# The decay-table spreads of a two-layer backbone, issued from ScalarE's DMA queue in place of GpSimd's

## The chip, the core and the metric

The kernel runs on one core of a Trainium2 chip. The metric is the device time of one execution in microseconds (us), as the median of several runs. Five engines work in parallel, each through its own instructions in a fixed order: TensorE (PE in the profile, with PEld for its weight loads), VectorE (DVE), ScalarE (ACT), GpSimd (POOL) and SyncE (SP). SP issues the loads of inputs and weights. A DMA is issued from the instruction list of one of these engines and is then carried out by the 16 DMA engines that all of them share.

## The reference, cut to what matters

The reference is a two-layer backbone on 256 latent tokens and 256 context tokens of width 1024. Each layer has an adaptive RMSNorm, three token mixers (a four-head retention in both directions, a short convolution, a multi-scale pooling), gates and an output projection, and then a hierarchical mixture of 16 experts. What the change touches is the decay of the retention:

```
rel = j[:, None] - j[None, :]
intra_decay = jnp.where(rel[None] >= 0.0,
                        jnp.exp(log_gamma[:, None, None] * jnp.maximum(rel, 0.0)[None]), 0.0)
scores = jnp.einsum('bnihd,bnjhd->bnhij', qc, kc) * intra_decay[None, None]
...
w_fwd = jnp.exp(log_gamma[0][:, None] * (n_tok - 1.0 - m)[None, :])
w_bwd = jnp.exp(log_gamma[1][:, None] * m[None, :])
```

Each score is multiplied by a power of the head's decay that depends only on the distance of the two tokens. So for each layer and head a row of 511 numbers (distances -255 to 255) is enough, and a second row of 511 for the decay from the context.

Ahead of the mixers, the conditioning `c @ w_ada[l] + b_ada[l]` gives shift, scale and gate; the mixers of layer 0 can't start without shift and scale.

## The kernel before, in words

All matrix products are done with operands split into a high and a low part: for each 128x1024 weight piece, ScalarE writes the rounded copy `wh` (L74) and VectorE the rest `wl` (L75), and TensorE does three products (L183 to L185). The pieces come in order through a ring of four buffers `raw` (L164, issued by SP); during the first stage ten more buffers `rawx` stand beside it.

**The first stage** (`src0`) runs before the first projection. `decays` computes the decay rows of all 8 layer-head pairs, 8 x 1022 numbers, and ACT writes them to `dg` in DRAM (L329). `ada_now` (L202 to L210) does four groups of the conditioning: 16 loads of 512 KB of `w_ada` (`in_wada`), issued by SP beside the input `x` (2 MB). Groups 0 and 2 come first, then `rstd`: squares, their sum, GpSimd's power (L371, `rs`) and VectorE's product of the whole input with it (L1293). Then follows `mix_norm0` for the first half of the 1024 channels: ACT's and DVE's `hf` (L430, L432), ACT's rounded copy `hT` (L433) and DVE's rest (L434). Groups 1 and 3 of the conditioning use split pieces (`wh`, `wl`); a row of each group is copied by ACT as `arow` (L205), turned by TensorE (L208) and added by DVE (`mod`, L210). When group 3 is in `mod`, `mix_norm0` does the second half. The last `hT` ends the stage. The whole order of each engine is fixed by a scheduler at build time.

**The decay tables.** `spread` (L333) copies the two rows of one layer and head 128 times in DRAM, from `dg` to `dw`: 256 rows of 2044 bytes, 511 KB. `table` (L340) then reads `dw` with a row step of 510 in place of 511 elements, so that each of the 128 partitions gets the row shifted by one: 384 KB into the tile `tab`. `scores` multiplies with `tab` (L563, L566, `pr`). There is one `tab` buffer for all heads, so each `table` waits until the scores of the head before are done.

`spread` is written in a block `tc.issue_after(mark[0].ins)`. `mark[0]` is the ScalarE instruction noted last: the `hT` copies of `mix_norm0`, the copies in `split`, a copy in `u_pool`. The first spread of layer 0 is written at the first head, the next three behind the first unit of heads 0 to 2, and the four of layer 1 one behind each `u_pool` of layer 0.

**The mixers** of layer 0 take up 75 to 560 us of the span; TensorE does one projection after the other there.

Of the kernel before, what the change touches and what calls it, by code (L numbers as in the profile page):

```python
# [78 lines left out]
def trunk(tc, io):  # L79
    nc = tc.nc  # L80
# [219 lines left out]
    ND = 2 * S - 1  # L300
    dg = dram.tile([NL * H, 2, ND], F32, name="dg")
    dw = dram.tile([NL * H, 2, P * ND], F32, name="dw")
# [30 lines left out]
    def spread(l, h):  # L333

        i = l * H + h
        with tc.issue_after(mark[0].ins):
            nc.gpsimd.dma_start(dw[i].rearrange("m (p j) -> p m j", j=ND),
                                dg[i].unsqueeze(0).to_broadcast([P, 2, ND]))

    def table(tab, l, h):  # L340
# [107 lines left out]
    def mixers(l, xsrc, x):  # L448
# [155 lines left out]
        for h in range(H):  # L604
            tab = hd.tile([P, 2, 384], F32, name="tab", tag="tab", bufs=1)
            if l == 0 and h == 0:
                spread(0, 0)
            table(tab, l, h)
            sg = []
            unit(u_qk, h, 0)  # L610
            if l == 0 and h < H - 1:
                spread(0, h + 1)
            if l == 0 and h == 0:
                late_consts()
            if last:
                for e in range(2):
                    unit(u_g, e, sg)
                    if h == 0:
                        late_norm(hd, range(4 * e, 4 * e + 4))
            unit(u_qk, h, 1)  # L620
            wv = [nextw(4), nextw(4)]
            after(DS[l], lambda tab=tab: scores(tab))
            after(DA[l], lambda h=h, sg=sg: attend(h, sg))
            for t2 in range(2):
                unit(u_v, t2, wv)
            if not last:
                for e in range(2):
                    unit(u_g, e, sg)
# [58 lines left out]
        for j in range(4):  # L687
            c = []
            unit(u_pool, j)
            if l == 0:  # L690
                spread(1, j)
            for i in range(3):
                unit(u_conv, j, i, c)
# [742 lines left out]
```

## Time and profile before

| what | value |
|---|---|
| median of 3 runs | 1699.37 us (1696.66 to 1704.01) |
| the profiled execution | 1695.72 us, of which the span is 1693.9 us |
| PE busy | 1623.9 us (96%) |
| DVE busy | 1348.3 us (80%) |
| ACT busy | 858.8 us (51%) |
| POOL busy | 69.9 us (4%) |
| DMA moved | 375.56 MB, mean 222 GB/s |

Busy times are those of the whole span. The page also cuts the span into 40 slices of 42 us: PE shows 5 and 7 tenths in the first two and 9 in most others, DMA 9 and 7 in the first two. Times in the rows further down are from the span's start; a row of the timeline gives start, duration, engine, line, what is written from what, and in brackets the idle time of the engine before it and what ended that.

### The profile page before, as it was taken

How to read it: one execution, taken by the hardware profiler on the slowest of the kernel's cores; microseconds unless marked ns; L12 is line 12 of the kernel's file. 1: busy time of each engine (PE TensorE's matmuls, PEld its weight loads, DVE VectorE, ACT ScalarE, POOL GpSimd, SP SyncE). 2: the span in 40 equal slices, each digit the busy share in tenths (PEclk: the TensorE clock that was granted, in tenths of full speed). 3: DMA queues.
4: the chain of work that ended last, by engine and by line, in shares of the span. 5: the costliest groups of instructions: out<-in, count | busy, mean ns of one | idle time of the engine just before them, and what ended most of it. 6: DMA issues, size and time to landing. Idle time of an engine off the chain costs nothing. (4 is left out here: it accounts for less than half of the span.)

```text
span 1693.9 us, 24511 instructions
## 1 busy us (share of the span) xinstructions
PE 1623.9 (96%) x8919; PEld 1367.7 (81%) x8919; DVE 1348.3 (80%) x2407; ACT 858.8 (51%) x1132; POOL 69.9 (4%) x101
## 2 busy tenths in 40 slices
PE   5799999999999997999999999999999989999996
PEld 1488888888888875888888878999999858888885
DVE  4577778977677458999999958779886688999995
ACT  3533332222222336777777745334444557787873
POOL 2000000000000001000000010000000010000000
PEclk8799999999999997999999999999999999999998
DMA  9733334454445526999999924435776579999991
GB/s 294 226 121 122 111 114 141 154 172 140 162 150 163 222 91 241 349 315 318 316 316 331 318 81 152 137 122 173 250 260 210 188 262 370 350 353 349 343 338 45
DMA packets 101870, 375.56 MB, mean 222 GB/s; under 512 B 11368, under 2 KB 11752, under 8 KB 101488
## 3 DMA queue, kind: packets, MB, share of 16 engines
q1 hardware_dynamic: 95472, 348.74, 59.9%
q0 software_dynamic: 5248, 19.92, 3.8%
q10 hardware_dynamic: 1024, 5.28, 0.8%
q8 instruction: 72, 1.18, 0.3%
q14 instruction: 54, 0.44, 0.1%
HBM read 369.67 MB, written 8.41 MB: 223 GB/s over the span
## 5 line engine op out<-in xcount | busy, mean ns | idle before, releaser
L74 ACT CAST wh<-raw 128x1024 fp32r<-128x1024 f32 x319 | 332.5, 1051 | 482.0 <-PE mm L184 274.7
L75 DVE TENSOR_TENSOR wl<-raw,wh 128x1024 fp32r<-128x1024 f32 x319 | 385.0, 1219 | 70.3 <-ACT wh L74 65.0
L74 ACT CAST wh<-rawx 128x1024 fp32r<-128x1024 f32 x247 | 257.3, 1053 | 114.0 <-PE mm L185 76.2
L183 PE MATMUL mm<-hT,wh 128*128 128x512 f32 (+1 forms) x896 | 307.4, 344 | 2.9 <-ACT wh L74 2.8
L75 DVE TENSOR_TENSOR wl<-rawx,wh 128x1024 fp32r<-128x1024 f32 x247 | 293.2, 1218 | 18.7 <-ACT wh L74 15.5
L184 PE MATMUL mm<-hT,wh 128*128 128x512 f32 (+1 forms) x896 | 306.4, 343 | 0.0
L185 PE MATMUL mm<-hT,wl 128*128 128x512 f32 (+1 forms) x896 | 304.8, 341 | 0.0
L230 DVE SCALAR_TENSOR_TENSOR acc<-raw,sv,acc 128x256 f32<-128x256 f32 x462 | 196.9, 476 | 8.9 <-DMA raw<-in_wada_dram 8.9
L183 PE MATMUL mm<-wh,X 128*128 128x512 f32 x512 | 200.6, 392 | 0.7 <-issue 0.7
L184 PE MATMUL mm<-wl,X 128*128 128x512 f32 x512 | 200.2, 391 | 0.0
L185 PE MATMUL mm<-wh,X 128*128 128x512 f32 x512 | 199.5, 390 | 0.0
L183 PEld LDWEIGHTS mm<-hT,wh 128*128 128x128 f32 x896 | 169.9, 190 | 21.8 <-ACT wh L74 3.6
L185 PEld LDWEIGHTS mm<-hT,wl 128*128 128x128 f32 x896 | 170.1, 190 | 19.1 <-issue 0.5
L184 PEld LDWEIGHTS mm<-hT,wh 128*128 128x128 f32 x896 | 170.1, 190 | 18.7 <-issue 0.7
L183 PEld LDWEIGHTS mm<-wh,X 128*128 128x128 f32 x512 | 96.4, 188 | 20.9 <-issue 1.3
L184 PEld LDWEIGHTS mm<-wl,X 128*128 128x128 f32 x512 | 96.4, 188 | 20.4 <-DVE wl L75 1.2
L185 PEld LDWEIGHTS mm<-wh,X 128*128 128x128 f32 x512 | 96.1, 188 | 19.8
L183 PE MATMUL mm<-wh,aTh 128*128 128x512 f32 x256 | 103.3, 404 | 5.4 <-ACT aTh L74 5.1
L184 PE MATMUL mm<-wl,aTh 128*128 128x512 f32 x256 | 100.3, 392 | 0.0
L185 PE MATMUL mm<-wh,aTl 128*128 128x512 f32 x256 | 96.3, 397 | 0.0
L1104 PE MATMUL yy<-GT,y 128*128 128x512 f32 (+1 forms) x384 | 94.2, 361 | 2.2 <-DVE xT L1108 2.1
L1104 PEld LDWEIGHTS yy<-GT,y 128*128 128x128 f32 x384 | 66.6, 188 | 14.5 <-issue 1.7
(346 smaller groups left out, 2613.6 us busy)
## 6 DMA issues: line engine op xcount, KB each, us to landing
rawx<-in_wmoe_dram SPq DMA_DIRECT2D x244, 512.0 KB, 5.3
raw<-in_wmix_dram SPq DMA_DIRECT2D x176, 512.0 KB, 3.9
raw<-in_wmoe_dram SPq DMA_DIRECT2D x140, 512.0 KB, 5.4
raw<-in_wada_dram SPq DMA_DIRECT2D x82, 512.0 KB, 3.8
rawx<-in_wada_dram SPq DMA_DIRECT2D x14, 512.0 KB, 12.4
dw<-dg POOLq DMA_DIRECT2D x8, 511.0 KB, 25.6
tab<-dw POOLq DMA_DIRECT2D x8, 384.0 KB, 4.0
h2d<-xs ACTq DMA_DIRECT2D x6, 512.0 KB, 5.3
```

Source lines behind the costliest of these rows:

```text
L74: nc.scalar.copy(hi, src)
L75: nc.vector.tensor_sub(lo, src, hi.bitcast(F32))
L183: nc.tensor.matmul(out, st[0], mv[0], start=start, stop=False)
L184: nc.tensor.matmul(out, st[0], mv[1], start=False, stop=False)
L185: nc.tensor.matmul(out, st[1], mv[0], start=False, stop=stop)
L230: nc.vector.scalar_tensor_tensor(acc[v], w[:, k], s, acc[v], op0=OP.mult, op1=OP.add)
L1104: nc.tensor.matmul(p_, y[i][:, c], GT, start=gi == 0 and i == 0, stop=gi == ng - 1 and i == 1)
```

## The change

One line: the DMA of `spread` is issued from ScalarE's instruction list and no longer from GpSimd's. `table` stays with GpSimd.

```
     with tc.issue_after(mark[0].ins):
-        nc.gpsimd.dma_start(dw[i].rearrange("m (p j) -> p m j", j=ND),
+        nc.scalar.dma_start(dw[i].rearrange("m (p j) -> p m j", j=ND),
                             dg[i].unsqueeze(0).to_broadcast([P, 2, ND]))
```

The place of the eight spreads in the program moves with it. On GpSimd before, from the program's start to the first two tables (`dl`, `tokid` are constants; the memsets are edges of the pooling and convolution tiles):

```order
L317 IOTA dl 8x511
L125 IOTA tokid 128x4
L337 DMA dw<-dg 128x2x511 x5
L371 TENSOR_TENSOR rs<-ms,neghalf 128x4
L337 DMA dw<-dg 128x2x511 x3
L342 DMA tab<-dw 128x2x384
L657 MEMSET b_2000 128x2x8
L658 MEMSET b_2000 128x2x8
L638 MEMSET u 128x2
L639 MEMSET u 128x2
L342 DMA tab<-dw 128x2x384
```

All eight spreads stand around the power `rs` of the first norm. On GpSimd after the change, the same stretch:

```order
L317 IOTA dl 8x511
L125 IOTA tokid 128x4
L371 TENSOR_TENSOR rs<-ms,neghalf 128x4
L657 MEMSET b_2000 128x2x8
L658 MEMSET b_2000 128x2x8
L638 MEMSET u 128x2
L639 MEMSET u 128x2
L342 DMA tab<-dw 128x2x384 x2
```

The eight spreads are gone from GpSimd, and the first table stands behind the four memsets. On ScalarE at the end of the first stage, the difference (`hT_97` is the rounded half of `hT`, `qr` and `yc_361` are pieces of q and k of head 0):

```order
 L433 CAST hT_97<-hf 128x512 x2
-L74 CAST wh<-raw 128x1024 x2
+L337 DMA dw<-dg 128x2x511
+L74 CAST wh<-raw 128x1024
 L514 CAST qr_407<-mm 128x256
-L74 CAST wh<-raw 128x1024
+L74 CAST wh<-raw 128x1024 x2
 L514 CAST yc_361<-mm 128x256
+L337 DMA dw<-dg 128x2x511
 L514 CAST qr_452<-mm 128x256
 L514 CAST yc_361<-mm 128x256
```

The first spread stands directly behind the last `hT` of the stage, the second some copies later, among those of head 0. The other six follow one by one: two among the copies of heads 1 and 2, and four each behind a copy of `u_pool` (L660). Besides, a `wh` changes places with the copy `qr_407`. SP's order is the same as before.

## Rows read from the trace of the kernel before

**Rows 1.** Busy time by stretch; columns named in the first row.

```profile
core 0: us, PE busy (x) PEld busy (x) DVE busy (x) ACT busy (x) POOL busy (x), PEclk, DMA share, GB/s
10.00:20.00 10.00, 8.90 (x27) 2.41 (x26) 5.91 (x9) 4.77 (x8) 2.67 (x4) 1.00 1.00 415
25.00:45.00 20.00, 6.90 (x18) 2.03 (x17) 8.28 (x16) 1.04 (x1) 3.70 (x4) 0.61 1.02 220
75.00:560.00 485.00, 482.34 (x2488) 410.74 (x2487) 373.47 (x787) 137.30 (x189) 7.49 (x19) 1.00 0.44 143
```

**Rows 2.** Timeline of GpSimd, 0 to 110 us.

```profile
17.33 3.70 POOL L337 DMA_DIRECT2D dw<-dg  x5 [15.85 <-DMA dg<-ev]
...
26.58 2.11 POOL L337 DMA_DIRECT2D dw<-dg  x3
73.61 0.74 POOL L342 DMA_DIRECT2D tab<-dw  x1 [44.91 <-DMA raw<-in_wmix_dram]
```

**Rows 3.** DMA queues, 20 to 60 us: packets, MB, share of 16 engines.

```profile
q1 hardware_dynamic: 1532, 5.70, 55.5%
q0 software_dynamic: 896, 4.19, 43.5%
```

**Rows 4.** Timeline of SP's queue, 0 to 110 us: the last first-stage loads.

```profile
18.95 1.59 SPq L164 DMA_DIRECT2D rawx<-in_wada_dram  x2
```

**Rows 5.** Timeline of ScalarE, 0 to 110 us.

```profile
46.98 1.04 ACT L74 CAST wh<-raw 128x1024 fp32r<-128x1024 f32 x1 [12.99 <-DMA raw<-in_wada_dram]
47.93 1.58 ACT L430 ACTIVATE hf<-x,mod,sca 128x256 f32<-128x256 f32 x3
...
53.17 1.05 ACT L74 CAST wh<-raw 128x1024 fp32r<-128x1024 f32 x1 [1.61 <-DMA raw<-in_wada_dram]
...
56.74 1.04 ACT L74 CAST wh<-rawx 128x1024 fp32r<-128x1024 f32 x1 [1.53 <-DMA rawx<-in_wada_dram]
59.30 1.05 ACT L74 CAST wh<-rawx 128x1024 fp32r<-128x1024 f32 x1 [1.51 <-DMA rawx<-in_wada_dram]
61.05 1.04 ACT L74 CAST wh<-raw 128x1024 fp32r<-128x1024 f32 x1 [0.71 <-DMA raw<-in_wmix_dram]
62.54 0.30 ACT L123 CAST swr<-con 128x128 fp32r<-128x128 f32 x1 [0.44 <-DMA con<-in_con_dram]
63.88 1.04 ACT L74 CAST wh<-raw 128x1024 fp32r<-128x1024 f32 x1 [1.04 <-DMA raw<-in_wmix_dram]
64.83 0.57 ACT L205 COPY arow<-mm 4x512 f32<-4x512 f32 x1
66.42 1.04 ACT L74 CAST wh<-raw 128x1024 fp32r<-128x1024 f32 x1 [1.01 <-DMA raw<-in_wmix_dram]
...
71.63 0.62 ACT L433 CAST hT<-hf 128x512 fp32r<-128x512 f32 x1 [0.18 <-DVE hf L432]
```

**Rows 6.** Timeline of VectorE, 0 to 100 us.

```profile
27.82 4.87 DVE L1293 TENSOR_TENSOR x<-x,st 128x512 f32<-128x512 f32 x8 [2.00 <-PE st L381]
32.61 0.16 DVE L266 SCALAR_TENSOR_TENSOR sca<-mod,vec 128x8 f32<-128x8 f32 x1
34.02 1.23 DVE L75 TENSOR_TENSOR wl<-raw,wh 128x1024 fp32r<-128x1024 f32 x1 [1.25 <-ACT wh L74]
...
50.04 1.90 DVE L434 TENSOR_TENSOR hT<-hf,hT 128x512 fp32r<-128x512 f32 x3 [13.51 <-ACT hT L433]
...
92.03 0.68 DVE L563 TENSOR_TENSOR pr<-st,tab 128x512 f32<-128x512 f32 x1
```

**Rows 7.** The spreads (L337), from issue to landing.

```profile
DMA to landing us min/median/max: 11.2/25.6/31.1
```

**Rows 8.** The tables, 60 to 140 us, from issue to landing.

```profile
DMA to landing us min/median/max: 3.7/3.8/3.8
```

**Rows 9.** DMAs that ScalarE issued, tile `h2d`: ns min/median/max.

```profile
L870 ACTq DMA_DIRECT2D h2d<-xs x6: 326/328/747, 635.7 to 1357.3; - x6
```

**Rows 10.** Waits, 75 to 360 us: total us, times, longest.

```profile
ACT wh L74 <- DMA raw<-in_wmix_dram: 2.8, 2, 1.8
```

## The prediction

> **What bounds the kernel now.** I read the busy time by stretch first, since the page's average (PE 96%) hides where TensorE is not busy. From 75 to 560 us it is busy 482.34 of 485 us, and DMA has a share of 0.44 [rows 1]: the mixers are bound by TensorE. The first stage is not. From 25 to 45 us TensorE is busy 6.90 of 20 us, VectorE 8.28 and ScalarE 1.04, while the DMA engines are full (1.02) and yet move only 220 GB/s, against 415 GB/s, also full, from 10 to 20 us [rows 1]. So the second question was what the DMA engines do there. GpSimd's timeline shows the eight spreads going out from 17.33 to 28.7 us [rows 2], and the queues between 20 and 60 us show two users: SP's loads, 5.70 MB in 55.5% of the time of 16 engines, and the spreads, 4.19 MB in 43.5% [rows 3]. The spreads thus take 0.435 x 40 = 17.4 us of all 16 engines, 2.2 us each, and SP's bytes take 22.2 us where 415 GB/s would need 13.7 us. Third, what waits for this: ScalarE's timeline. Its copy at 46.98 us had stood 12.99 us for a load of `w_ada`; later copies of this stage waited 1.61, 1.53, 1.51, 0.71, 0.44, 1.04 and 1.01 us for loads too [rows 5]. All of the first stage's loads were issued by 20.5 us [rows 4], so they were late in flight and not late in issue. Nothing that needs a spread waits in this stage: the first table is issued at 73.61 us [rows 2], the first product with it starts at 92.03 us [rows 6]. The spreads are early by tens of microseconds and are paid for by loads that are not.
>
> **The change, part by part.**
>
> *Removed from the first stage: 4.19 MB of spreads.* By the order, none is issued before the last `hT` of the stage, which ended at 71.63 + 0.62 = 72.25 us [rows 5]. What SP has in flight at 20 us then runs by itself. Even if I charge it with all of SP's 5.70 MB [rows 3], which includes pieces for the mixers, at 415 GB/s [rows 1] it is through by 20 + 13.7 = 33.7 us; the pieces that ScalarE wants first are near the front of that.
>
> What is late next is VectorE: the product of the input with the norm's power runs from 27.82 us, and `sca`, which the first `hf` need, ends at 32.61 + 0.16 = 32.77 us [rows 6]. Nothing in this chain waits for a load. So the `hf` that started at 47.93 us [rows 5] start at 32.77 us: 15.2 us earlier. If the two copies ahead of them should come with the last of the 5.70 MB, at 33.7 us and 1.04 us each, the `hf` start at 35.8 us, and 12.1 us are left; that is the lower end of this term.
>
> From there to `arow` at 64.83 us ScalarE took 16.9 us, 6.8 us of it waiting for loads (the first six waits named above) [rows 5]. Not all of that comes back, as VectorE follows behind: from the first rounded `hT`, some 2.1 us after the `hf` begin, it has 1.90 us of `hT`, four `wl` of 1.23 us, another `hT` and a `mod` [rows 6], about 7.7 us, which ends at 42.6 us at the earliest; TensorE's products with the last piece come behind that, in the same order as before. I give these and the waits of three engines for each other 2 to 4 us, so `arow` stands at 44.6 to 46.6 us instead of 64.83 - 15.2 = 49.6 us. The term lies between 0 and 6.8 us; I take 3 us, the lower end of what the walk leaves.
>
> Behind `arow` there is one more wait of 1.01 us [rows 5], and TensorE's granted clock, 0.61 in the starved stretch [rows 1], which is its lower level of 1.2 GHz for most of it; whether it is higher in a denser stage no row tells. I set both at nothing, with 2 us to either side. Sum of the first stage: 15.2 + 3 = 18.2 us.
>
> *Added to ScalarE: eight issues.* The nearest row is ScalarE's own issue of 512 KB, 0.33 to 0.75 us [rows 9]: 2.6 to 6.0 us in all. ScalarE is busy 137.30 of 485 us in the mixers [rows 1], so nothing of it reaches TensorE as long as a `wh` is ready before its turn. Behind the first issue are queued a `wh` and the copy `qr` of head 0, behind the second the copy of k; TensorE waits for these only if the copies come later than its products before them. I take 0; if all of it were on the path, 6 us. The first spread waits for `dg`, long since landed; the second stands behind a load that SP issued many microseconds earlier. GpSimd loses eight issues of some 0.7 us at a time when little waits for it.
>
> *Moved into the mixers: the eight transfers.* Each takes 2.2 us of all DMA engines, 17.4 us together, in a stretch whose DMA share is 0.44 and where ScalarE's copies waited for mixer pieces only 2.8 us in 285 [rows 1, 3, 10]. I take 0, up to 3 us. Weighed against this is the Trainium skill (DMA: Bandwidth & Descriptors, Queues, rings and completion order): each DMA engine takes turns between the queue rows that have work, so a piece in flight beside a spread gets about half the engine, wherever the spread was issued. The trace agrees (220 GB/s beside the spreads, 415 before). By that rule the sum would be the one above only while the pieces are ahead of their use, and at most 17.4 us smaller if none is; that is the bound that the last rival goes beyond.
>
> *Added wait: the first table.* It was ready long before, and now hangs on a spread that goes out at about 72.25 - 18.2 = 54.1 us. Before, the last `hT` and the first product with the table were 92.03 - 72.25 = 19.8 us apart [rows 5, 6], and that distance is TensorE's work, which stays. In it must fit the issue (0.5 us), the landing of the spread, GpSimd's issue of the table (0.74 us) [rows 2] and its landing (3.8 us) [rows 8]: 14.8 us are left for the spread. Its landing took 11.2 us at best, 25.6 us in the median [rows 7], but that was with seven others and the loads in full engines; the best is the nearest to one spread alone. So the table is in time, by 3.6 us at least. By the Trainium skill's fit for one DMA (same page, Anatomy of one DMA), 2.0 us plus bytes over 436 GB/s, a spread alone would land in an estimated 3.2 us, and the slack would be 11.6 us; no row here shows a spread alone. The other tables wait for the scores of the head before, and their spreads go out a head earlier or more.
>
> So the profiled execution, 1695.72 us, becomes 1677.5 us. The median of the runs lies 3.65 us above that execution; against it I forecast 1699.4 - 18.2 = 1681.2, **1681 us**.
>
> **Rivals.**
>
> *The table takes the place of the load.* ScalarE's spread lands as late as the eight did in the median, 25.6 us: the scores wait 25.6 - 14.8 = 10.8 us, and with the worst, 31.1 us, 16.3 us. The gain shrinks to 7.4 or 1.9 us: 1692 to 1697.5 us. For it: the spread writes to DRAM in 2044-byte rows, and the weight pieces run beside it. Against: one spread needs 2.2 us of the engines. 9%.
>
> *The loads are slow by themselves.* If what remains in the stage runs at the 247 GB/s of 9.89 MB in 40 us that all users had together [rows 3], SP's 5.70 MB take 23 us instead of 40, the last copies end at 43 us instead of 60, and what ScalarE wants in the middle gains about half of the 18 us: 1690 us. For it: DMA was full in both stretches. Against: 415 GB/s with the same kind of loads just before. 8%.
>
> *The spreads hurt where TensorE is the bound* (slower). From 75 us on every microsecond that a weight piece is late counts in full, once its lead over its use is gone; before, the lead sufficed. If a spread costs there what it cost in the first stage in elapsed time, 40 us for eight, 5 us each, the mixers lose 40 us, and the net is 22 us slower: 1721 us. It decides from 18.2 / 8 = 2.3 us of TensorE's time per spread, which is just what one spread takes of the engines; a ScalarE held by each issue for that long, with the `wh` behind it, would do the same. Against: a DMA share of 0.44, four buffers ahead, and issues below 0.75 us. 7%.
>
> *The change does not do what it says*: it does, by the order; the eight stand on ScalarE.
>
> **How the numbers follow.** The forecast has 76%, with its own range from 1675 (the second term whole, 2 us from the clock) to 1688 us (first term at 12.1, the second at nothing, a little lost to the issues); the rivals have 9, 8 and 7%. About 0.5%, 8.5 us, is what a measurement of this kernel can tell from no change, so faster means below 1691 us: the forecast and half of the second rival, 80%. No change holds the first rival and the other half, 13%. Slower holds the last, 7%. The range that leaves out 2 in 10 goes from 1675 to 1693 us: it takes in the forecast's own and the nearer part of the first two rivals.
>
> **What would show it.** Right: between 25 and 45 us of the changed kernel no spread, the GB/s near 400 until all loads are in, no wait of ScalarE for `w_ada` above 2 us, the `hf` near 33 us, the last `hT` near 54 us, the first spread right behind it and the first `pr` near 74 us with TensorE and not the table ending its wait; from there on both traces the same distance apart, and 482 of 485 us of TensorE again. Wrong: `pr` waiting for the table (first rival), loads still late with the engines empty of spreads (second), gaps of TensorE at the places of the eight spreads or an issue on ScalarE above 2 us (third). Of the terms, the 3 us between `hf` and `arow` is the weakest.

## The result and the profile after

| kernel | median of its runs | range | ratio to the kernel before, 95% interval |
|---|---|---|---|
| before, beside it | 1698.01 us | 1696.27 to 1704.01 | |
| changed | 1681.01 us | 1673.98 to 1683.32 | 0.9887 [0.9848, 0.9926] |

The changed kernel is faster by 17.0 us at the median (forecast: 18.2). The profiled execution took 1683.32 us, its span 1681.5 us against 1693.9.

First the DMA engines from 20 to 60 us, in 40 slices of 1 us: their busy share in tenths, what they moved, and the queues (answering to [rows 3]).

```profile
DMA  9999999996000003899998994997603846848988
GB/s 410 401 414 414 410 401 410 418 406 270 20 0 0 0 0 74 332 428 423 311 381 332 406 414 176 299 332 184 238 29 41 303 180 121 215 135 176 279 221 114
...
q1 hardware_dynamic: 2541, 9.36, 64.4%
q10 hardware_dynamic: 368, 0.72, 8.5%
```

SP's loads run at 401 to 418 GB/s and are through at 30 us; then the engines have nothing to do until 35 us. Of the spreads, now on q10, only 0.72 MB is left here, behind 51.8 us; the 4.19 MB on q0 are gone. The stretch that answers to [rows 1], and two later ones:

```profile
core 0: us, PE busy (x) PEld busy (x) DVE busy (x) ACT busy (x) POOL busy (x), PEclk, DMA share, GB/s
25.00:45.00 20.00, 15.39 (x54) 5.80 (x53) 17.98 (x28) 11.35 (x17) 1.93 (x1) 0.83 0.68 260
75.00:560.00 485.00, 481.76 (x2439) 409.68 (x2439) 362.68 (x769) 132.50 (x181) 7.51 (x19) 0.99 0.47 153
105.00:110.00 5.00, 3.05 (x24) 2.88 (x23) 5.00 (x13) 2.03 (x5) 0.00 (x0) 0.92 0.49 159
```

From 25 to 45 us TensorE is busy 15.39 instead of 6.90 us, ScalarE 11.35 instead of 1.04. ScalarE's timeline (answering to [rows 5]):

```profile
27.21 1.04 ACT L74 CAST wh<-raw 128x1024 fp32r<-128x1024 f32 x1 [1.51 <-DMA raw<-in_wada_dram]
33.41 1.58 ACT L430 ACTIVATE hf<-x,mod,sca 128x256 f32<-128x256 f32 x3 [5.16 <-DVE sca L266]
...
45.57 0.57 ACT L205 COPY arow<-mm 4x512 f32<-4x512 f32 x1 [2.56 <-PE mm L202]
...
51.77 0.62 ACT L433 CAST hT<-hf 128x512 fp32r<-128x512 f32 x1 [0.18 <-DVE hf L432]
51.80 0.63 ACTq L337 DMA_DIRECT2D dw<-dg  x1
```

The copy that had stood 12.99 us for a load now stands 1.51 us, and what ends the wait ahead of the `hf` is VectorE's `sca`. The `arow` waits for TensorE and no longer for loads. GpSimd's first table, VectorE's `sca` and its first product with that table (answering to [rows 2, 6]):

```profile
58.94 0.96 POOL L342 DMA_DIRECT2D tab<-dw  x1 [5.40 <-DMA dw<-dg]
```

```profile
33.22 0.15 DVE L266 SCALAR_TENSOR_TENSOR sca<-mod,vec 128x8 f32<-128x8 f32 x1
...
71.74 0.68 DVE L563 TENSOR_TENSOR pr<-st,tab 128x512 f32<-128x512 f32 x1
```

The product starts 20.29 us earlier than before and is not made to wait by the table, which landed at 68.1 us. It is late by VectorE's own order: VectorE had stood 3.03 us, up to 65.50 us, for a load of `w_ada` that SP issued at 57.38 us, 0.4 us behind the second spread, and works from there to the product without a pause. TensorE waits 0.87 us for the product:

```profile
65.50 0.62 DVE L228 TENSOR_SCALAR acc<-raw,sv 128x256 f32<-128x256 f32 x2 [3.03 <-DMA raw<-in_wada_dram]
```

```profile
72.56 0.35 PE L183 MATMUL st<-yc 128*128 128x256 f32 x1 [0.87 <-DVE pr L563]
```

In again, the second run of this kernel below, these two waits are 2.31 and 0.16 us. The spreads' own rows, issue (ns) and landing (answering to [rows 7, 9]):

```profile
L337 ACTq DMA_DIRECT2D dw<-dg x8: 537/538/633, 51.8 to 299.6; - x8
DMA to landing us min/median/max: 7.1/7.2/7.5
```

The landing of the first table, 20 to 60 us:

```profile
tab<-dw POOLq DMA_DIRECT2D x1, 384.0 KB, 9.2
```

The first stage gains 19.9 us (end of the last `hT`: 72.25 before, 52.39 after). The span gains 12.4 us. So this execution gives 7.5 us back: the first product behind the mixers (L771) starts at 550.13 us, 18.2 us earlier than before (568.30), which leaves 1.7 us lost in the mixers and 5.8 us behind them. The next rows show a loss in the mixers: in turn ScalarE's issue of the third spread, SP's load that meets it, VectorE, which wants this load, and TensorE.

```profile
91.00 0.54 ACTq L337 DMA_DIRECT2D dw<-dg  x1
```

```profile
92.22 0.33 SPq L164 DMA_DIRECT2D raw<-in_wada_dram  x1
```

```profile
98.63 0.48 DVE L230 SCALAR_TENSOR_TENSOR acc<-raw,sv,acc 128x256 f32<-128x256 f32 x1 [2.84 <-DMA raw<-in_wada_dram]
...
107.91 0.68 DVE L598 TENSOR_TENSOR yf<-st,sg 128x512 f32<-128x512 f32 x1
```

```profile
108.73 0.47 PE L529 MATMUL st<-qr,swr 128*128 128x256 f32 x2 [1.95 <-DVE yf L598]
```

The spread goes out at 91.00 us and the load at 92.22; VectorE's accumulation for a later group of the conditioning stands 2.84 us for it, the `yf` behind it in VectorE's order comes late, and TensorE waits 1.95 us. It is busy 3.05 of the 5 us from 105 on, and its granted clock is 0.92 there.

Behind the mixers the loss goes with the clock. The row of the changed kernel, and that of before around the same products:

```profile
548.00:568.00 20.00, 20.00 (x97) 17.47 (x96) 7.04 (x15) 6.04 (x11) 0.00 (x0) 0.74 0.80 309
```

```profile
566.00:586.00 20.00, 20.00 (x125) 17.61 (x124) 8.29 (x17) 7.79 (x13) 0.00 (x0) 1.00 0.87 342
```

TensorE is busy all the time in both, but the clock is 0.74 in one: a stretch of 10.2 us at the lower level of 1.2 GHz, which begins right behind the small products of L771. Before ran the same products at 1.00. At half the clock 10.2 us are worth up to 5.1 of the 5.8 us (an estimate). Further on both kernels have stretches at the lower level: 36 us in all behind the mixers of before, 53 us in the changed kernel, these 10.2 us among them.

### The profile page after: what moved, and what is told of

Same layout as the page of the kernel before. It is cut to its first block, busy times and chain, and to the rows that moved or that the text cites. A ratio compares the mean times of both kernels' runs of the same rounds, so it can differ in the third digit from the quotient of the medians.

```text
span 1681.5 us, 24507 instructions
## 1 busy us (share of the span) xinstructions
PE 1626.4 (97%) x8919; PEld 1373.0 (82%) x8919; DVE 1347.9 (80%) x2407; ACT 858.1 (51%) x1132; POOL 64.1 (4%) x93
## 5 line engine op out<-in xcount | busy, mean ns | idle before, releaser
L1104 PEld LDWEIGHTS yy<-GT,y 128*128 128x128 f32 x384 | 66.6, 188 | 14.5 <-issue 1.7
```

Of the source, the lines that this page charges most:

```text
L1104: nc.tensor.matmul(p_, y[i][:, c], GT, start=gi == 0 and i == 0, stop=gi == ng - 1 and i == 1)
```

## The experiments

Two theories. **A**: only the place in time counts; the spreads took the DMA engines' time from the first stage's loads, and any late issue cures it. **B**: GpSimd's queue itself is the price, and another queue the cure.

Milestones of the profiled executions, in us; "mixers" runs from the last `hT` to the first L771, "rest" from there to the end of the span:

| kernel | early spreads | end of last hT | first L771 | span | mixers | rest |
|---|---|---|---|---|---|---|
| before | 8 | 72.25 | 568.30 | 1693.9 | 496.1 | 1125.6 |
| changed | 0 | 52.39 | 550.13 | 1681.5 | 497.7 | 1131.4 |
| again | 0 | 51.55 | 546.83 | 1673.8 | 495.3 | 1127.0 |
| nospread | none at all | 50.75 | 543.70 | 1669.1 | 493.0 | 1125.4 |
| pool_late2 | 0 | 52.34 | 550.08 | 1681.3 | 497.7 | 1131.2 |
| half | 4 | 60.44 | 552.67 | 1683.7 | 492.2 | 1131.0 |
| double | 16 | 97.28 | 591.48 | 1716.7 | 494.2 | 1125.2 |
| gap3 | 3, of ScalarE | 53.06 | 545.61 | 1675.2 | 492.6 | 1129.6 |
| idle1 | 1, of ScalarE | 53.64 | 546.35 | 1671.3 | 492.7 | 1125.0 |

**The change again, in more runs** (again; no edit).

> The changed kernel once more. In its first trace the first product with a table came 20.3 us earlier than before, but the span was only 12.4 us shorter: 3.3 us went near 105 to 113 us of the span (a gap of TensorE of 2 us, then 3.4 us of the lower clock), some 5 us in a stretch of 10.2 us at the lower clock from 553 to 563 us. If the first loss belongs to the third spread (its transfer beside a load of w_ada), it stands here again at the same place, 3 to 4 us. If the second is chance of the clock, it is absent or elsewhere here, and the span is 1676 to 1678 us; if it belongs to the change, it is here again and the span is 1680 to 1683 us. Median of the runs 1677 to 1683 us.

Measured 1675.76 us (1673.83 to 1678.28), ratio 0.9882 [0.9858, 0.9906], a little below the 1677 to 1683 us that I had expected. The wait of TensorE near 107 us is there again, and belongs to the change:

```profile
106.87 0.48 PE L529 MATMUL st<-qr,swr 128*128 128x256 f32 x2 [1.89 <-DVE yf L598]
```

The low clock right behind the mixers lasts 3.4 us here and not 10.2, and the rest takes 1127.0 us instead of 1131.4 with the same program: that part varies between executions.

**The spreads late, but from GpSimd** (pool_late). The edit is against the kernel before: a small GpSimd instruction reads the ScalarE copy that `mark` names, and the spread is issued behind it.

```
+    probe = cst.tile([P, 8], F32, name="probe")
...
-        i = l * H + h
-        with tc.issue_after(mark[0].ins):
+        i = l * H + h; late = nc.gpsimd.tensor_scalar(probe[:, i:i + 1], mark[1][:, 0:1], 0.0, None, op0=OP.mult)
+        with tc.issue_after(late.ins):
             nc.gpsimd.dma_start(dw[i].rearrange("m (p j) -> p m j", j=ND),
...
```

> All spreads stay in GpSimd's queue, as before, but each is issued only when the ScalarE copy is done behind which the change put it (a small GpSimd instruction that reads that copy's result stands ahead of each spread). Theory A, the place in time is what counts: hf near 33 us, last hT near 53 us, time 1678 to 1685 us, as with the change. Rival B, the queue is what counts (a spread from the software queue holds the DMA engines longer than one from ScalarE's): in the mixers the spreads then land later than 7.2 us, the first table is late, and at least half of the gain is missing: 1690 us or more.

Measured 1688.74 us, ratio 0.9949 [0.9932, 0.9967]: at first sight half of B. But its first stage was as short as the change's (the last `hT` ends at 50.44 us), and most of the loss lay in the mixers, 505.2 us against 495.3 in again, without a gap that holds it: products of 512 columns followed each other every 233 ns from 400 to 540 us, 227 ns in all kernels before. The tile `probe` takes 32 bytes of each partition and moves the tiles allocated behind it by as much, so the run told nothing about queues. It was repeated without the tile:

```
-    probe = cst.tile([P, 8], F32, name="probe")
-        i = l * H + h; late = nc.gpsimd.tensor_scalar(probe[:, i:i + 1], mark[1][:, 0:1], 0.0, None, op0=OP.mult)
+        i = l * H + h; late = nc.gpsimd.tensor_scalar(se[:, i, 0:1], mark[1][:, 0:1], 0.0, None, op0=OP.mult)
```

> The same as pool_late (all eight spreads back in GpSimd's list, each behind the ScalarE copy that holds it in the changed kernel), but the one number per partition that the small GpSimd instruction writes goes into a tile that exists already (se, not used any more at that time), so no tile of the kernel changes its address. Theory A (only the place in time matters, not which engine issues): first hf near 33 us, last hT near 51 us, matmuls in the mixers again 227 ns apart as in all kernels but pool_late, and 1674 to 1682 us. Theory B (GpSimd's queue itself costs, and with it the slower matmuls of pool_late): 233 ns apart again and 1686 to 1692 us.

Measured 1680.07 us (1677.35 to 1683.20), ratio 0.9891 [0.9868, 0.9913], as the change's 0.9887; the milestones are the change's within 0.2 us. The landing of its spreads and their first issue from GpSimd:

```profile
DMA to landing us min/median/max: 6.3/6.9/7.6
```

```profile
53.11 0.99 POOL L337 DMA_DIRECT2D dw<-dg  x1
```

A holds and B falls: late from GpSimd is worth the same as late from ScalarE. On GpSimd `issue_after` with a ScalarE copy had set no order (the eight spreads stood around `rs`); on ScalarE it does. That is how a change of queue became one of place. The meeting of the third spread with a load is there with GpSimd too: the spread goes out from GpSimd at 91.48 us, SP's load at 91.52, and TensorE waits 2.59 us for `yf`.

**No spreads** (nospread). The tables are read from `dg` and not from `dw`; nearly as many bytes as before.

```
-            nc.scalar.dma_start(dw[i].rearrange("m (p j) -> p m j", j=ND),
-                                dg[i].unsqueeze(0).to_broadcast([P, 2, ND]))
...
-        src = dw[l * H + h, :, P - 1:P - 1 + P * (ND - 1)].rearrange("m (p j) -> p m j", j=ND - 1)
+        src = dg[l * H + h].unsqueeze(0).to_broadcast([P, 2, ND])
```

> No spreads at all: the tables are read from the 511-number rows themselves, each partition the same row, 384 KB as before, so the scores are multiplied by a wrong table. All else stands where it stood. This is the price of what the change leaves in the mixers. If the third spread costs 3.3 us there and the others nothing: 1677 to 1679 us, no gap of TensorE near 105 us. If the moved spreads cost nothing: the time of the changed kernel, 1681 us. If all eight cost as much as the third: under 1665 us.

Measured 1672.54 us (1670.99 to 1673.37), ratio 0.9863 [0.9832, 0.9894]. That lies in none of the three ranges, which I had counted from the first 1681 us. What the eight late spreads still cost is some 3 us of the median of again. TensorE has no gap near 105 us:

```profile
105.00:110.00 5.00, 5.00 (x42) 4.91 (x41) 2.91 (x6) 2.37 (x4) 0.00 (x0) 1.00 0.18 71
```

The order of TensorE's work is no rival for the gap: it is the same from the first instruction to the last in pool_late2, which has the gap, and in nospread, which has not.

**Twice the spreads, early** (double; one copy of the two is read by nobody; the edit is against the kernel before).

```
-            nc.gpsimd.dma_start(dw[i].rearrange("m (p j) -> p m j", j=ND), ...
+            for d in (dw2, dw):
+                nc.gpsimd.dma_start(d[i].rearrange("m (p j) -> p m j", j=ND), ...
```

> The kernel before with each of the eight spreads written twice, the second time to a tensor that nobody reads: 16 transfers at the old early place, from GpSimd. Theory A (the price in the first stage is the time that the spreads take of the DMA engines, 2.2 us each): eight more cost 17 us or somewhat more there, the first wait for a load of w_ada ends near 60 to 65 us, and the whole takes 1712 to 1722 us. Rival (the price is GpSimd's early issues, or the loads are slow by themselves): below 1706 us, since the engine waits for nothing in that stage.

Measured 1718.74 us (1717.11 to 1719.78), ratio 1.0123 [1.0100, 1.0146]: 20 us more than before, as A says. ScalarE's waits for loads:

```profile
33.09 1.04 ACT L74 CAST wh<-raw 128x1024 fp32r<-128x1024 f32 x1 [8.12 <-DMA raw<-in_wada_dram]
47.02 1.04 ACT L74 CAST wh<-raw 128x1024 fp32r<-128x1024 f32 x1 [12.88 <-DMA raw<-in_wada_dram]
...
63.22 1.04 ACT L74 CAST wh<-rawx 128x1024 fp32r<-128x1024 f32 x1 [5.78 <-DMA rawx<-in_wada_dram]
72.84 1.04 ACT L74 CAST wh<-rawx 128x1024 fp32r<-128x1024 f32 x1 [8.58 <-DMA rawx<-in_wada_dram]
```

One detail was expected wrongly: the first long waits end where they did before (33 and 47 us), not at 60 to 65. The later copies pay instead, at 63 and 73 us. The same row of DMA use, as long as spreads are in flight:

```profile
25.00:72.00 47.00, 18.49 (x52) 5.59 (x51) 15.11 (x25) 8.71 (x13) 9.54 (x12) 0.61 1.01 213
```

Full engines at 213 GB/s for 47 us, as at 220 GB/s for 20 us before [rows 1].

**Half of them early** (half).

```
-            nc.gpsimd.dma_start(dw[i].rearrange("m (p j) -> p m j", j=ND),
+            (nc.gpsimd if l == 0 else nc.scalar).dma_start(dw[i].rearrange("m (p j) -> p m j", j=ND),
```

> The four spreads of layer 0 are issued early by GpSimd, as in the kernel before; the four of layer 1 late by ScalarE, as in the change. So four transfers of some 2.2 us of all DMA engines, 8.7 us, stand in the first stage, and none meets a load near 91 us. If the price goes with the number of spreads (eight moved the last hT by 20.5 us, eight more in the kernel double moved the whole by another 20): the last hT near 62 us and 1680 to 1688 us. If the stretch of 4 to 5 us in which the DMA engines of the changed kernel are empty (29 to 34 us) first takes up about two spreads: the last hT near 55 to 57 us and 1674 to 1680 us.

Measured 1684.76 us (1680.99 to 1685.66), ratio 0.9916 [0.9890, 0.9941], and the last `hT` ends at 60.44 us.

```profile
33.58 1.04 ACT L74 CAST wh<-raw 128x1024 fp32r<-128x1024 f32 x1 [9.32 <-DMA raw<-in_wada_dram]
41.77 1.04 ACT L74 CAST wh<-raw 128x1024 fp32r<-128x1024 f32 x1 [7.14 <-DMA raw<-in_wada_dram]
```

The empty stretch of the DMA engines takes up nothing, since the spreads run ahead of it, beside the loads. From again (0 early spreads) to half (4), before (8) and double (16) the last `hT` moves by 8.9, 11.8 and 25.0 us: 2.2, 3.0 and 3.1 us a spread.

**Three spreads earlier, from ScalarE** (gap3), behind the `arow` of group 2 at 23.43 us, the last one no longer near 91 us.

```
-        ada_now(2, tmp)
+        ada_now(2, tmp); [spread(0, i) for i in range(3)]
...
-        nc.scalar.copy(r[0:n4], p_)
+        mark[0] = nc.scalar.copy(r[0:n4], p_)
...
-                spread(0, 0)
+                pass
...
-            if l == 0 and h < H - 1:
+            if l == 0 and 3 <= h + 1 < H:
```

> The first three spreads of layer 0 go out from ScalarE at about 24.6 us, behind the row copy of group 2, where the DMA engines are about to run out of work (in the changed kernel they stood nearly still from 30.5 to 35 us); the other five stay where the change put them. If the third spread's transfer is what cost 3.3 us near 105 us: that gap is gone, three spreads of 2.2 us fill the pause and push the loads behind it by some 2 us, of which the copies hide most: 1676 to 1680 us. Rival, the first stage is again held up by spreads (8.7 us of transfers for four, in the share of the eight before): hf later than 36 us and the time 1683 us or more.

Measured 1676.29 us (1674.49 to 1680.43), ratio 0.9887 [0.9854, 0.9920]: no better than the change. The mixers are 2.7 us shorter than in again, the first stage 1.5 us longer (ScalarE's next copy stands 1.44 us behind the three issues, and two later ones wait 1.35 and 0.80 us for mixer pieces: the spreads meet the loads after all), and this execution had longer stretches at the lower clock behind the mixers (rest 1129.6).

**One spread in the empty stretch, none at 91 us** (idle1).

```
-    nc.scalar.copy(hi, src)
+    WH[:] = [nc.scalar.copy(hi, src)]
...
-                ops = [(svr, 4, a) for a in wsplit(src)]
+                ops = [(svr, 4, a) for a in wsplit(src)]; mark[:] = WH; [spread(0, j) for j in range(1) if (g, i) == (3, 0)]
...
-                spread(0, 0)
+                spread(0, 1)
...
-            if l == 0 and h < H - 1:
-                spread(0, h + 1)
+            if l == 0 and h in (0, 2):
+                spread(0, 2 + h // 2)
```

> The changed kernel with the first three spreads at other places of ScalarE's list: the first directly behind the third copy wh of the first stage, near 27 us, so that it meets the stretch from 29 to 34 us in which the DMA engines have nothing to do; the second where the first stood, behind the last hT near 51 us; the third where the second stood, near 57 us, and none near 91 us beside the load of w_ada. The fourth and the four of layer 1 are as in the change. If the third spread's meeting with that load costs the changed kernel 3 to 5 us, and a spread in the empty stretch costs nothing: no gap of TensorE at 105 us and 1671 to 1674 us, as the kernel without spreads (1672.5). If the loss near 105 us belongs to the mean of the executions only now and then, or the first spread still meets the loads: 1675 to 1678 us as the change.

Measured 1674.59 us (1673.10 to 1679.21), ratio 0.9873 [0.9847, 0.9898]: the lowest median of the kernels with spreads, but it lies between the two ranges that I had written and its interval overlaps the change's, so that a gain of 1 us over it isn't shown. What is shown is the mechanism: the spread goes out where the DMA engines fall empty, none goes out near 91 us, and TensorE's gap is gone.

```profile
27.65 0.63 ACTq L337 DMA_DIRECT2D dw<-dg  x1
```

```profile
105.00:110.00 5.00, 4.96 (x43) 4.79 (x42) 4.53 (x10) 2.23 (x4) 0.00 (x0) 1.00 0.48 155
```

The mixers take 492.7 us, as without spreads (493.0). Its first stage ended 2 us later than that of again, but that came from ahead of the spread: the norm's power `rs` started at 27.32 us and not near 25.

**Tiles moved by some bytes** (shim32, and with other sizes shim64, shim128, shim256), on the changed kernel:

```
+    shim = cst.tile([P, 8], F32, name="shim"); nc.gpsimd.memset(shim, 0.0)
```

> The changed kernel with one unused tile of 32 bytes per partition, set to zero by GpSimd at the very start, allocated at the place where pool_late has its tile; nothing else changes but the addresses of the tiles behind it. If the addresses are what made pool_late's matmuls 233 ns apart and not 227: 233 ns here too, with the spreads issued from ScalarE, and 1684 to 1692 us. If it was the queue or the extra waits of GpSimd: 227 ns and 1674 to 1679 us as the changed kernel.

> As shim32, but the unused tile has 64 bytes per partition, so wh and wl of the mixers are written 64 bytes lower than in the changed kernel (address 160832 of the partition for the first wh, against 160896 in the change and 160864 in shim32). If matmuls are slower where these tiles do not start at a multiple of 64 bytes: 227 ns apart again and 1674 to 1680 us. If it is a multiple of 128 bytes that counts, or any shift against the other tiles: 233 ns as in shim32 and 1686 to 1691 us.

> As shim64 with 128 bytes per partition: the first wh starts at 160768, a multiple of 256, where it was an odd multiple of 128 in the change. If only multiples of 64 or 128 count: 227 ns and 1674 to 1680 us, no different from the change. If the granule is larger still: below 227 ns and below 1670 us.

> As shim64, with 256 bytes per partition: the first wh starts at 160640, where only address bits from 256 up differ from the change. If the time between matmuls follows the low bits of the addresses of wh and wl: 227 ns as in the change (0 bytes: 227.4, 32: 233.4, 64: 229.0, 128: 232.4) and 1674 to 1680 us. If it follows the distance to the other tiles, whatever the low bits: another value again, 229 to 233 ns and 1682 to 1690 us.

| unused bytes per partition | 0 (changed) | 32 | 64 | 128 | 256 |
|---|---|---|---|---|---|
| ns from start to start, 400 to 540 us | 227.3 | 233.4 | 229.0 | 232.4 | 227.4 |
| median us | 1681.01, 1675.76 | 1688.84 | 1683.70 | 1688.78 | 1678.45 |

The first of these rows is the mean distance of the starts of successive products of 512 columns (gaps above 300 ns left out). TensorE's order is the same in all five. The mean of one such product (with a modelled end), 120 to 540 us, of the changed kernel and of shim32:

```profile
L183 PE MATMUL mm<-hT,wh 128*128 128x512 f32 x389 | 153.3, 394 | 0.0
```

```profile
L183 PE MATMUL mm<-hT,wh 128*128 128x512 f32 x382 | 152.4, 399 | 0.0
```

shim32 repeats pool_late's loss with no queue involved (1688.84 and 1688.74 us), which settles what that run had been about. My explanation by multiples of 64 bytes failed with shim64 (229.0, not 227) and still more with shim128. With 256 bytes the old value is back: of the five offsets, the two that agree in the lower 8 bits of the address are the fast ones. Which two tiles get in each other's way stays open.

## Why the prediction was right

The forecast was 1681 us, the measured medians are 1681.01 and 1675.76 us. The mechanism held: the spreads were in the way of the loads, and the first stage got shorter by the 17.4 us that they had taken of the engines and a little more. That the first median agrees to the microsecond is partly luck. The first stage gave 19.9 us in place of 18.2, and the profiled execution, forecast at 1677.5 us, took 1683.32: 1.7 us went in the mixers and 5.8 us behind them, where the sum had nothing. By its steps:

- **The first hf, 15.2 us earlier.** 47.93 to 33.41 us is 14.5 us (15.3 in again), and the wait ahead is for `sca`, as the prediction had it. The loads were through at 30 us, inside the bound of 33.7.
- **From hf to arow, 3 us (0 to 6.8).** 16.9 us became 12.2 us in both executions, so 4.7 us: the right range, mis-sized by 1.7 us. I had kept the lower end of what the walk along VectorE left. One reading behind the term was wrong: the waits of 0.71, 0.44 and 1.04 us were for mixer pieces and constants, which SP issued from 35 us on and not by 20.5 us. From `arow` on another 0.6 us came back.
- **The rate.** With the spreads gone the same loads went at 401 to 418 GB/s. (The 220 GB/s that the prediction sets against 415 as a sign of turns are loads and spreads together; what bears on the turns is their shares of the engines' time, 55.5 and 43.5% [rows 3].) The rival of loads slow by themselves is out; half and double show that the first stage's length goes with the spreads' number, at 2.2 us each for four, the time each takes of all DMA engines, and some 3 us each for more.
- **The first table.** Spread issued at 51.80 us, table at 58.94, landed 9.2 us later at 68.1, first product at 71.74: a slack of 3.6 us, as the sum had it, but by two errors that cancel. The spread landed in 7.1 us and not 11.2; the table took 9.2 us and not 3.8, with the second spread (57.01 us) in flight beside it. The Trainium skill (DMA: Bandwidth & Descriptors, Anatomy of one DMA) would have the spread land in an estimated 3.2 us. That fit is stated for transfers that GpSimd issues; pool_late2's, issued from there, took 6.3 to 7.6 us, and the eight of the change 7.1 to 7.5 us, in a stretch with a DMA share of 0.47. No run shows a spread quite alone. The nearest is idle1's first, whose packets ran from 29.2 to 32.4 us, beside loads only up to 30.9 us: 6.2 us from issue to landing. The measurement decides, and the slack of 11.6 us worked out from the page was not there.
- **Eight issues on ScalarE, 0.** 0.54 to 0.63 us each, in the bracket of 0.33 to 0.75; in the mixers no wait of TensorE ends with one.
- **Eight transfers in the mixers, 0 (up to 3 us).** Against before the mixers took 0.8 us less in again and 1.7 us more in the first profile. But without spreads they take 2.3 to 4.7 us less than with them, so the transfers are not free. Most of it is one meeting, of the third spread with a load of `w_ada` at 92 us: idle1, half and gap3, without it, take 492.2 to 492.7 us. Before had losses of its own in their place: TensorE waited 2.2 us in all for VectorE's `bs` (0.3 in nospread), and ahead of the longer of the two waits VectorE had stood 2.00 us for a load of `w_ada`, with no spread in flight (two lines of before below). I had reckoned with an average (DMA share 0.44) and looked only at ScalarE's weight pieces; the late reader was VectorE, which accumulates from another load of the same queue. The third rival needed 2.3 us for each spread; one of eight came near it (1.95), and the rival fell.
- **The clock, 0 (2 us to either side).** In the first stage the clock rose (0.61 to 0.83) with no separate price to be read. Not foreseen: that the stretches of low clock behind the mixers grow, from 36 us in all in before to 53 in the changed kernel, 10.2 of them at a place where before has none. The rest takes 1125 to 1127 us with 36 to 40 us of low clock and 1130 to 1131 with 53 to 55: 4 to 6 us, more than the 2 us allowed. They vary with one program (40 us in again); this may be why two sets of runs of the same kernel differ by 5 us.

```profile
151.70 3.26 DVE L230 SCALAR_TENSOR_TENSOR acc<-raw,sv,acc 128x256 f32<-128x256 f32 x8 [2.00 <-DMA raw<-in_wada_dram]
```

```profile
155.35 0.39 PE L183 MATMUL yy<-yc,yp 128*128 128x256 f32 x1 [1.42 <-DVE bs L582]
```

What stays open: why some executions stay longer at the lower clock behind the mixers, and whether idle1 is truly faster than the change.

## What to carry to other kernels

Where DMA engines are full at half the rate that they had a little earlier, as here (220 against 415 GB/s), see whether something not urgent is beside something urgent: look for the transfer whose reader is furthest away, and move it in time; here the queue that issued it made no difference. When it moves, look up which single load each copy will meet, since an average share hides the meeting. And when an experiment adds a tile, even of 32 bytes, first see whether the distance between the matmuls is the same in both traces.

## What the runs showed of the hardware that I had not expected

- A matmul's pace depends on where the tiles lie: 227 to 233 ns per product of 512 columns by an unused tile of 32 bytes per partition, 8 to 13 us of this kernel, about half of what the change brought.
- GpSimd went on issuing without a wait up to nine spreads; in double the tenth and each later one waited 3.0 to 6.5 us until an earlier had landed. Whether the chip or the program's semaphores set that limit no run tells.

```profile
17.80 3.70 POOL L338 DMA_DIRECT2D dw<-dg  x5 [16.31 <-DMA dg<-ev]
...
27.55 2.79 POOL L338 DMA_DIRECT2D dw<-dg  x4
33.34 0.69 POOL L338 DMA_DIRECT2D dw<-dg  x1 [2.99 <-DMA dw<-dg]
38.45 0.69 POOL L338 DMA_DIRECT2D dw<-dg  x1 [4.43 <-DMA dw<-dg]
```
